# Feed-forward products: low parts of weights on VectorE alone, explicit order on all engines, a bank's steps between the next bank's weight tiles

## The chip, the cores and the metric

One core of one Trainium2 chip runs the whole program in one launch. The metric is the device time of that launch in microseconds: the median of three runs before is 1933.09 us (1932.76 to 1934.46).

## The reference

Two blocks over 256 tokens of 1024 features, batch 1, all in fp32. The first block has four layers, each with an attention (differential, stick-breaking, sliding window, differential) and a feed-forward with a causal convolution of three taps; it ends with a norm. The second block has a gated feed-forward, a mixing layer, an attention over a memory of 256 rows, and a second gated feed-forward. The parts that the change touches:

```python
def conv_gated_ffn(h, w_up, conv_w, conv_b, w_down):      # D_FF = 2752, layers 0 to 3
    u = h @ w_up                                          # [256, 2 * 2752]
    u = causal depthwise conv of width 3 over the tokens (u, conv_w) + conv_b
    gate, val = jnp.split(u, 2, axis=-1)
    return (jax.nn.silu(gate) * val) @ w_down

def swiglu(h, w_gate, w_up, w_down):                      # D_FF_2 = 2816, second block, twice
    return (jax.nn.silu(h @ w_gate) * (h @ w_up)) @ w_down
```

The input of each is a root-mean-square norm of the residual, and the first block's output is added to the residual `x = x + conv_gated_ffn(...)`.

## The kernel before

**Products.** Activations lie feature-major: 8 row tiles of 128 features by 256 tokens. Each fp32 product is made of three matmuls in a rounded format (`fp32r`): with weights w = hi + lo and activations a = ah + al, it sums hi·ah, hi·al and lo·ah (`fm`, L177). A *weight tile* is 128 x 128, so a weight tile is three matmuls of 256 columns. A *unit* is 8 weight tiles (128 x 1024 in SBUF), a *chunk* two units, 1 MB of the weight stream in DRAM, which is laid out in the order of use: 564 units in all.

**The weight stream.** `take` (L159) hands out tiles; at the middle of each unit it calls `split_to` for the unit three ahead (`AHEAD`), that is 20 tiles before its first use. `split_next` (L139) makes the high part `whi` with a copy on ScalarE (L153) and, a number of tiles later (`lag`, 4), the low part `wlo` with a subtraction (L156) on the engine that the string `lo_engines` names in turn: V for VectorE, P for GpSimd. The high and the low parts have 5 buffers each, the chunks 4; `dma_to` issues the transfer of a chunk on the sync queue (SP) three chunks ahead of the one that is split.

**Side work.** `spawn` puts a generator on a list; each number that it yields says how many weight tiles are to pass before its next step, and `tick`, called after every tile, runs the steps that are due. So the place of a step in the program is set in tiles of TensorE's work.

**Order on the engines.** `order()` (L1176) opens a region: without an argument every engine (the sync queue too) runs its instructions in the order of the program; with `{PE}` TensorE alone does, and a planner in the compiler places the instructions of the other engines by its own costs. Before, everything was explicit up to the last part of layer 0's attention output (`out_proj`) and from the cross-attention's output to the lead of the last feed-forward; the rest, all feed-forwards but that lead, had TensorE alone in explicit order.

**A feed-forward layer** (`ffn_layer`, L709). The up part has 22 *banks* of PSUM (`ubank`, three buffers): bank i holds the gate and value columns i, two products of 256 tokens, 16 weight tiles; bank 21 is one column (64 gate and 64 value features), 8 tiles. Banks 0 and 21 come first and advance together, row tile by row tile (the *lead*, 24 tiles), while the last row tiles of the normed input are being made. The norm's factor r comes by `start_norm`: after 12 tiles a product with a matrix of ones sums the squares `accss` over the partitions, and two activations on ScalarE make r. For each bank VectorE takes it out of PSUM times r (`ub`, L741), ScalarE starts the convolution (`y`, L746, once for gate and once for value), VectorE adds two taps to each (L748, four instructions), ScalarE does the silu (`gs`, L255), VectorE the product `g` (L755), ScalarE its high part `gh` (L759), VectorE its low part `gl` (L761). In the program these stand in one row after the bank's matmuls. The down part (`down`, L774) has 8 columns of 22 tiles, the first two together; row tile 21 has 64 rows and needs two matmuls, with high and low part stacked. Each column is added to the residual and goes through `feed` (L334) into the next layer's input. `lo_engines` is "VP" in the up part and "VVP" in the down part.

**The gated feed-forwards** (`swiglu`, L784) are alike, without taps, 22 banks of 16 tiles and 22 row tiles in the down part; "VVP" throughout. Beside the first, the memory is loaded and normed (`load_mem`, L1208); `final_r` (L1158) makes the factors of the norms. The last one's down part (`finish`, L860) is token-major.

Of the kernel before, what the change touches and what calls it, by code (L numbers as in the profile page):

```python
# [10 lines left out]
F32 = mybir.dt.float32  # L11
F32R = mybir.dt.float32r
AF = mybir.ActivationFunctionType
# [6 lines left out]
P = 128  # L20
T = 256
# [9 lines left out]
# Attention layers: weight tiles passed before the scores and before each later step of a block, the engines of the low  # L31
# parts of the weights, of the high copies of q and k, and of the other parts of q and of k.
# [40 lines left out]
class Act:  # L73
    """Activations in high and low parts. A stacked row tile has 64 rows: h holds the high part above the low part."""
# [5 lines left out]
class Net:  # L80
    def __init__(self, tc, ctx, A):
# [27 lines left out]
        self.bt_bufs = 3  # L109

# [22 lines left out]
    def split_to(self, u):  # L133
        while self.n_split <= min(u, N_UNITS - 1):
            self.dma_to(self.n_split // 2 + 3)
            gen = self.split_next(1024, 4)
            self.spawn(gen, next(gen))

    def split_next(self, step, lag=0):  # L139
        """the next unit of weights, in high and low parts, step columns at a time"""  # L140
# [35 lines left out]
    # feature-major products, row tile by row tile: out[128 features, 256 tokens] += W[rows kt, cols]^T act[kt]  # L176
# [17 lines left out]
    # token-major products: out[t][128 tokens, 256 or 512 features]  # L194
# [47 lines left out]
    def pin(self):  # L242
        """One table set serves every Exp and Ln until the next Silu."""
# [65 lines left out]
    def start_norm(self, f=None, tok=False, delay=10):  # L309
        """r of the tokens (in self.r, times f in self.rq, by token in self.rtok), after some weight tiles"""  # L310
# [27 lines left out]
    def out_proj(self, name, idx, act, rows, evac, order=tuple(range(KT)), urgent=False):  # L338
        """The first six columns advance together, row tile by row tile, while the last heads finish."""
# [31 lines left out]
    # one block of two score rows [128, 2, 384] (query tiles 0: 128 keys, 1: 256 keys)  # L371
# [10 lines left out]
    def q_parts(self, pool, ps):  # L382
        """[:, j]: the high part of head j in its own 64 rows, the low part in the other 64"""
# [13 lines left out]
    def k_parts(self, pool, ps, tag="", bufs=2):  # L397
        """the high part of head j in both halves of [:, j], and the low parts of both heads"""
# [15 lines left out]
    def head_product(self, out, j, q, queries, k, keys, keys_first=False):  # L414
        """queries x keys of head j (or keys x queries)"""
# [37 lines left out]
    def transposed(self, pool, a, ps):  # L453
        """a [128 q, 384] -> psum [128 k, 384]: keys 0..127 of 256 queries, keys 128..255 of queries 128.."""
# [3 lines left out]
    def load_bias(self, pool, kind, chans):  # L458
        """[query i, channel, key c]: bias at distance 128 + i - c"""
# [17 lines left out]
    # differential attention, one head  # L477
# [48 lines left out]
    # stick-breaking attention, a block of two heads  # L526
# [45 lines left out]
    # plain softmax attention with a Toeplitz bias, a block of two heads  # L572
# [55 lines left out]
    def units(self, name, idx, cols, act, kts=tuple(range(KT)), rows=None):  # L628
        """several output blocks, each in its own bank, advancing together"""
# [80 lines left out]
    def ffn_layer(self, layer, xf, nxt):  # L710
# [3 lines left out]
        with ExitStack() as st:  # L714
# [6 lines left out]
            for t in ub:  # L721
                nc.gpsimd.memset(t[:, :, 0:2], 0.0)
            self.lo_engines = "VP"
            self.start_norm(delay=12)
# [3 lines left out]
            self.fm([(b[:, p * T:p * T + T], name, layer, cols, p == 0)  # L728
                     for b, parts in zip(banks, lead) for p, cols in enumerate(parts)], xf, range(KT))
            for n, i in enumerate(order):  # L730
                parts = up_cols(i)
                np_ = len(parts)
                if n < 2:
                    bank = banks[n]
                else:
                    bank = self.ubank()
                    for p, cols in enumerate(parts):
                        self.fm([(bank[:, p * T:p * T + T], name, layer, cols, True)], xf, range(KT))
                r = self.r
# [10 lines left out]
                m = P if np_ == 2 else 64  # L750
# [15 lines left out]
            self.lo_engines = "VVP"  # L766
# [17 lines left out]
    def swiglu(self, tag, xt, rget, down):  # L784
        """down(g) takes the last product."""
        nc = self.nc
        with ExitStack() as st:
# [5 lines left out]
            self.lo_engines = "VVP"  # L793
# [6 lines left out]
            if self.manual:  # L800
                self.order({mybir.EngineType.PE})
# [529 lines left out]
```

## Time and profile before

| what | value |
|---|---|
| runs | 1932.76, 1933.09, 1934.46 us |
| span of the profiled execution, first to last instruction | 1932.7 us (its mean granted TensorE clock 0.980) |
| TensorE matmuls busy | 1849.3 us, 96%, 14082 instructions |
| weight loads (PEld) busy | 1761.5 us, 91% |
| VectorE (DVE) busy | 1342.0 us, 69% |
| ScalarE (ACT) busy | 1096.4 us, 57% |
| GpSimd (POOL) busy | 735.3 us, 38% |
| DMA | 314.87 MB, mean 163 GB/s |

Busy shares are means over the whole span, over stages with different limits. A matmul's record is longer than the distance to the next start, since matmuls are pipelined; the pace is read from the starts. "Idle before" an instruction is put down to what ended it.

### The profile page before, as it was taken

To read this page: it belongs to the slowest core of one execution; us is meant where nothing else is said; L and a number is where in the kernel's file an instruction comes from. 1 tells how busy PE (TensorE), PEld (TensorE's weight loads), DVE (VectorE), ACT (ScalarE), POOL (GpSimd) and SP (SyncE) were. 2 spreads that over 40 slices of the span, in tenths; PEclk is the share of its full clock that TensorE was granted. 3 is DMA by queue.
4 is the path that set the end of the run, shared out by engine and by line. 5 is a ranking of instruction groups with operands and counts; after the bars stand their busy time and mean duration, and the time that the engine had idled before them with its cause. 6 is when DMAs were issued, how large, how long until landed. Compare 5 with 4: busy or idle time off the path is not lost.

```text
span 1932.7 us, 35139 instructions
## 1 busy us (share of the span) xinstructions
PE 1849.3 (96%) x14082; PEld 1761.5 (91%) x14082; DVE 1342.0 (69%) x2093; ACT 1096.4 (57%) x1906; POOL 735.3 (38%) x433
## 2 busy tenths in 40 slices
PE   8999999999998999999999999989999999989998
PEld 7889989988987988999899899889999999989996
DVE  6778884676899557788757689967763655756653
ACT  6665664666555556566556655555544545655543
POOL 5453333554333321433344343334323454342222
PEclk9999999999998999999999999999999999999999
DMA  8634445433444452344544344454555454434452
GB/s 279 225 132 167 170 167 195 153 109 131 150 152 157 175 180 83 139 169 173 196 175 153 131 148 151 150 185 172 200 176 195 150 189 154 153 121 175 175 182 79
DMA packets 56994, 314.87 MB, mean 163 GB/s; under 512 B 5616, under 2 KB 19344, under 8 KB 20992
## 3 DMA queue, kind: packets, MB, share of 16 engines
q1 hardware_dynamic: 55872, 310.84, 45.4%
q8 instruction: 111, 1.82, 0.4%
q0 software_dynamic: 384, 1.04, 0.1%
q10 hardware_dynamic: 576, 0.75, 0.1%
q14 instruction: 51, 0.42, 0.1%
HBM read 311.52 MB, written 5.29 MB: 164 GB/s over the span
## 4 chain that ended last, share of the span: by engine, by line
PE 44%; DVE 10%; ACT 2%; issue 1%; POOL 1%; DVEq 0%; ACTq 0%; POOLq 0%
PE u L174 41%; DVE y L748 4%; PE s L174 3%; DVE wlo L156 2%; DVE ub L741 1%; DVE xtl L271 1%; ACT whi L153 1%; DVE x L836 1%; DVE g L755 0%; ACT gh L759 0%; ACT y L746 0%; DVE f L835 0%; PE s L456 0%; POOL wlo L156 0%; DVE accss L287 0%
## 5 line engine op out<-in xcount | busy, mean ns | idle before, releaser
L156 POOL TENSOR_TENSOR wlo<-stage,whi 128x1024 fp32r<-128x1024 f32 x245 | 598.1, 2442 | 1039.3 <-ACT whi L153 938.3
L174 PE MATMUL u<-xth,wlo 128*128 128x256 f32 x2704 | 776.8, 287 | 17.8 <-DVE wlo L156 9.5
L174 PE MATMUL u<-xth,whi 128*128 128x256 f32 x2704 | 782.7, 290 | 3.0 <-ACT xth L270 2.9
L174 PE MATMUL u<-xtl,whi 128*128 128x256 f32 x2704 | 770.5, 285 | 3.2 <-DVE xtl L271 3.2
L153 ACT ACTIVATE whi<-stage 128x1024 fp32r<-128x1024 f32 (+1 forms) x568 | 591.0, 1045 | 289.7 <-PE u L174 224.8
L156 DVE TENSOR_TENSOR wlo<-stage,whi 128x1024 fp32r<-128x1024 f32 (+1 forms) x323 | 420.2, 1303 | 204.7 <-ACT whi L153 201.9
L174 PEld LDWEIGHTS u<-xth,wlo 128*128 128x128 f32 x2704 | 523.9, 194 | 30.0 <-DVE wlo L156 18.0
L174 PEld LDWEIGHTS u<-xth,whi 128*128 128x128 f32 x2704 | 524.5, 194 | 9.5 <-ACT xth L270 3.3
L174 PEld LDWEIGHTS u<-xtl,whi 128*128 128x128 f32 x2704 | 524.5, 194 | 4.5 <-DVE xtl L271 3.6
L748 DVE SCALAR_TENSOR_TENSOR y<-ub,vec,y 128x256 f32<-128x256 f32 x344 | 276.1, 846 | 32.9 <-ACT y L746 29.3
L174 PE MATMUL u<-gh,whi 128*128 128x256 f32 x880 | 256.1, 291 | 18.3 <-DVE ub L741 18.3
L174 PE MATMUL u<-gh,wlo 128*128 128x256 f32 x880 | 255.9, 291 | 0.7 <-DVE wlo L156 0.7
L174 PE MATMUL u<-gl,whi 128*128 128x256 f32 x848 | 241.6, 285 | 0.0
L174 PEld LDWEIGHTS u<-gh,whi 128*128 128x128 f32 x880 | 169.6, 193 | 23.9 <-DVE ub L741 19.1
L174 PEld LDWEIGHTS u<-gh,wlo 128*128 128x128 f32 x880 | 168.8, 192 | 6.1 <-issue 1.6
L174 PEld LDWEIGHTS u<-gl,whi 128*128 128x128 f32 x848 | 163.2, 193 | 0.0
L746 ACT ACTIVATE y<-ub,vec 128x256 f32<-128x256 f32 x172 | 93.7, 593 | 39.3 <-DVE ub L741 39.3
L174 PE MATMUL u<-oh,whi 128*128 128x256 f32 x384 | 112.3, 292 | 1.4 <-DVE x L367 1.0
L174 PE MATMUL u<-ol,whi 128*128 128x256 f32 x384 | 108.2, 282 | 2.1 <-DVE ol L523 2.0
L174 PE MATMUL u<-oh,wlo 128*128 128x256 f32 x384 | 108.2, 282 | 0.0
L759 ACT ACTIVATE gh<-g 128x256 fp32r<-128x256 f32 x88 | 36.8, 418 | 103.7 <-DVE g L755 100.6
L271 DVE SCALAR_TENSOR_TENSOR xtl<-x,vec,xth 128x256 fp32r<-128x256 f32 x88 | 79.9, 913 | 18.8 <-ACT xth L270 18.7
(235 smaller groups left out, 2457.9 us busy)
## 6 DMA issues: line engine op xcount, KB each, us to landing
stage<-w SPq DMA_DIRECT2D x280, 1024.0 KB, 4.8
bt<-bt_d SPq DMA_DIRECT2D x24, 256.0 KB, 5.2
bt_d<-rows_d SPq DMA_DIRECT2D x1, 2048.0 KB, 12.2
stage<-w SPq DMA_DIRECT2D x4, 256.0 KB, 6.5
stage<-w SPq DMA_DIRECT2D x2, 512.0 KB, 7.0
bt_d<-rows_d SPq DMA_DIRECT2D x2, 512.0 KB
bt_d<-rows_d SPq DMA_DIRECT2D x1, 1024.0 KB
mem<-memT SPq DMA_DIRECT2D x8, 128.0 KB, 4.2
```

The source lines that it names most:

```text
L153: nc.scalar.activation(hi[:, s], src[:, s], AF.Copy)
L156: eng.tensor_tensor(lo[:, s], src[:, s], hi[:, s].bitcast(F32), OP.subtract)
L174: self.nc.tensor.matmul(out, lhsT, rhs, start=start, stop=stop, skip_group_check=True)
L271: nc.vector.scalar_tensor_tensor(l[:, j], src, gcol, h[:, j].bitcast(F32), op0=OP.mult, op1=OP.subtract)
L741: nc.vector.tensor_tensor(u[:, 0:np_, 2:258], bank[:, 0:np_ * T].rearrange("p (a t) -> p a t", t=T), r.unsqueeze(1).to_broadcast([P, np_, ...
L746: nc.scalar.activation(y[:, p], u[:, p, 2:258], AF.Identity, scale=cv(i, p, 2), bias=cv(i, p, 3))
L748: nc.vector.scalar_tensor_tensor(y[:, p], u[:, p, tap:tap + T], cv(i, p, tap), y[:, p], op0=OP.mult, op1=OP.add)
L759: nc.scalar.activation(gh[:m, i], g[:m], AF.Copy)
L836: nc.vector.tensor_tensor(self.x[:, c], self.x[:, c], self.f[:, c], OP.add)
```

## The change

The up and down parts of all six feed-forwards, and the leads, run in explicit order on all engines (`order()` at their start; after the down part TensorE alone again, save after the last). `lo_engines` is "V" in them, and `lag` is 6, back to 4 at their end. A bank's steps become a generator `gate`, spread over the next bank's tiles by its yields: for a layer `ub` at the bank's end, `y` after 2 tiles, the taps of the gate after 4, silu and the taps of the value after 5, `g` and `gh` after 9, `gl` after 13. Bank 0 starts as soon as r is there, bank 21 eight tiles after the lead. A layer's `start_norm` comes after 27 tiles, not 12. A row tile of the down part counts as done when its `gl` has been issued. Comments are left out of the changed file, so its line numbers differ.

```diff
+        self.lag = 4
-            gen = self.split_next(1024, 4)
+            gen = self.split_next(1024, self.lag)
...
 def ffn_layer(self, layer, xf, nxt):
-            self.lo_engines = "VP"
-            self.start_norm(delay=12)
+            self.order()
+            self.lo_engines = "V"
+            self.lag = 6
+            self.start_norm(delay=27)
...
+            def gate(n, i, bank):
+                np_ = len(up_cols(i))
+                m = P if np_ == 2 else 64
+                while self.r is None:
+                    yield 1
                 u = ub[n % 3]
                 nc.vector.tensor_tensor(
                     u[:, 0:np_, 2:258], bank[:, 0:np_ * T].rearrange("p (a t) -> p a t", t=T),
-                    r.unsqueeze(1).to_broadcast([P, np_, T]), OP.mult)
+                    self.r.unsqueeze(1).to_broadcast([P, np_, T]), OP.mult)
+                yield 2
                 y = pool.tile([P, 2, T], F32, tag="y", name="y")
                 for p in range(np_):
                     nc.scalar.activation(y[:, p], u[:, p, 2:258], AF.Identity, scale=cv(i, p, 2), bias=cv(i, p, 3))
+                def taps(p):
                     for tap in (1, 0):
                         nc.vector.scalar_tensor_tensor(y[:, p], u[:, p, tap:tap + T], cv(i, p, tap), y[:, p],
                                                        op0=OP.mult, op1=OP.add)
+                yield 2
+                taps(0)
+                yield 1
                 gs = pool.tile([P, T], F32, tag="gs", name="gs")
                 self.silu(gs[:m], y[:m, 0])
+                if np_ == 2:
+                    taps(1)
+                yield 4
...
                 nc.scalar.activation(gh[:m, i], g[:m], AF.Copy)
+                if n == 21:
+                    self.pin()
+                yield 4
                 low = gl[:, i] if np_ == 2 else gh[64:, i]
                 nc.vector.tensor_tensor(low, g[:m], gh[:m, i].bitcast(F32), OP.subtract)
-            self.pin()
+                ga.done.add(i)
+            def start(n, i, bank, delay=0):
+                gen = gate(n, i, bank)
+                if delay:
+                    self.spawn(gen, delay)
+                else:
+                    self.spawn(gen, next(gen))
...
+                    start(n, i, bank)
+                else:
+                    start(n, i, banks[n], 8 * n)
-            self.lo_engines = "VVP"
...
             self.down("ffn_w_down", layer, ga, order, after, rows)
+            self.lag = 4
+            self.order({mybir.EngineType.PE})
 def down(self, name, idx, act, order, after, rows=None):
-        act.done.update(range(22))
 def swiglu(self, tag, xt, rget, down):
-            self.lo_engines = "VVP"
+            self.order()
+            self.lo_engines = "V"
+            self.lag = 6
...
+            def gate(i, bank):
+                while self.r is None:
+                    yield 1
...
+                yield 3
                 gs = pool.tile([P, T], F32, tag="gs", name="gs")
                 self.silu(gs, u[:, 0])
+                yield 3
...
-            if self.manual:
-                self.order({mybir.EngineType.PE})
...
             down(ga)
+            self.lag = 4
+            if tag != "ffn2":
+                self.order({mybir.EngineType.PE})
 def finish(self, act, out):
                 parts = self.take(4)
+                while kt not in act.done:
+                    self.tick(True)
```

## Rows read from the trace of the kernel before

**Rows 1.** The core: us of the span, mean granted TensorE clock.
```profile
core 0: 1932.7 us, clock 0.980
```

**Rows 2.** Windows: us, busy and count by engine, clock, DMA; layers 0-3, gated, lead.
```profile
139.44:340.66 201.22, 193.32 (x1557) 189.25 (x1555) 149.81 (x209) 116.40 (x175) 77.35 (x38) 0.99 0.49 171
469.90:688.10 218.20, 201.44 (x1557) 193.54 (x1555) 166.45 (x209) 117.06 (x177) 76.28 (x39) 0.96 0.45 160
783.79:989.18 205.39, 196.51 (x1557) 192.03 (x1555) 154.15 (x209) 116.99 (x177) 77.93 (x39) 0.97 0.46 165
1114.63:1330.20 215.57, 200.31 (x1557) 192.45 (x1556) 169.21 (x211) 119.00 (x181) 79.11 (x42) 0.98 0.45 162
1335.63:1521.98 186.35, 186.35 (x1555) 186.35 (x1554) 113.03 (x132) 96.16 (x144) 61.05 (x31) 1.00 0.52 186
...
1726.35:1746.48 20.13, 16.96 (x91) 16.40 (x92) 15.16 (x21) 8.51 (x18) 10.12 (x9) 0.67 0.31 105
```

**Rows 3.** Waits: who waited for whom, us in total, times, longest.
```profile
PE u L174 <- DVE ub L741: 18.3, 4, 5.3
...
PE s L174 <- DVE accss L287: 15.4, 7, 4.0
...
PE u L174 <- DVE wlo L156: 11.0, 28, 1.6
```

**Rows 4.** Timeline of TensorE, layer 1, end of up part: start, us, what, idle.
```profile
614.39 0.38 PE L174 MATMUL u<-gh,wlo 128*128 128x256 f32 x1 [0.34 <-DVE wlo L156]
620.12 0.58 PE L174 MATMUL u<-gh,whi 128*128 128x256 f32 x1 [5.34 <-DVE ub L741]
620.50 0.41 PE L174 MATMUL u<-gl,whi 128*128 128x256 f32 x1
620.71 0.41 PE L174 MATMUL u<-gh,wlo 128*128 128x256 f32 x1
620.93 0.41 PE L174 MATMUL u<-gh,whi 128*128 128x256 f32 x1
```

**Rows 5.** Timeline of VectorE, layer 1, one bank of the up part and more.
```profile
564.58 1.23 DVE L156 TENSOR_TENSOR wlo<-stage,whi 128x1024 fp32r<-128x1024 f32 x1
565.72 3.83 DVE L748 SCALAR_TENSOR_TENSOR y<-ub,vec,y 128x256 f32<-128x256 f32 x4
569.65 0.43 DVE L755 TENSOR_TENSOR g<-gs,y 128x256 f32<-128x256 f32 x1
570.57 0.42 DVE L761 TENSOR_TENSOR gl<-g,gh 128x256 fp32r<-128x256 f32 x1 [0.48 <-ACT gh L759]
570.91 0.68 DVE L741 TENSOR_TENSOR ub<-u,r 128x512 f32<-128x512 f32 x1
571.51 1.23 DVE L156 TENSOR_TENSOR wlo<-stage,whi 128x1024 fp32r<-128x1024 f32 x1
572.66 1.27 DVE L748 SCALAR_TENSOR_TENSOR y<-ub,vec,y 128x256 f32<-128x256 f32 x3
```

**Rows 6.** Timeline of GpSimd, the same stretch.
```profile
566.88 2.39 POOL L156 TENSOR_TENSOR wlo<-stage,whi 128x1024 fp32r<-128x1024 f32 x1 [4.54 <-ACT whi L153]
```

**Rows 7.** Groups of ScalarE by line and form: busy, mean ns, idle before.
```profile
L153 ACT ACTIVATE whi<-stage 128x1024 fp32r<-128x1024 f32 x560 | 586.1, 1051 | 289.7 <-PE u L174 224.8 <-issue 53.1 <-ACT whi L153 3.6
L746 ACT ACTIVATE y<-ub,vec 128x256 f32<-128x256 f32 x172 | 93.7, 593 | 39.3 <-DVE ub L741 39.3
L759 ACT ACTIVATE gh<-g 128x256 fp32r<-128x256 f32 x84 | 35.2, 419 | 103.7 <-DVE g L755 100.6
L255 ACT ACTIVATE gs<-y 128x256 f32<-128x256 f32 x84 | 35.1, 418 | 74.1 <-DVE y L748 74.0
```

**Rows 8.** Timeline of TensorE, layer 1, the norm's ones-product.
```profile
478.20 1.22 PE L174 MATMUL s<-accss,ones 128*128 128x256 f32 x2 [3.82 <-DVE accss L287]
```

**Rows 9.** Timeline of TensorE, layer 1, the row tile of 64 rows.
```profile
639.38 0.28 PE L174 MATMUL u<-gh,whi 128*128 128x256 f32 x1
...
640.13 0.28 PE L174 MATMUL u<-gl,whi 128*128 128x256 f32 x1
```

More of the change, by code (lines that the diff above doesn't have):

```diff
@@ L727, in ffn_layer @@
             banks = [self.ubank(), self.ubank()]
[L728 to L739, printed above, removed]
+            def gate(n, i, bank):
[3 more added lines that the diff above has]
+                    yield 1
                 u = ub[n % 3]
@@ L749, in ffn_layer @@
                                                        op0=OP.mult, op1=OP.add)
-                m = P if np_ == 2 else 64
+                yield 2
+                taps(0)
+                yield 1
                 gs = pool.tile([P, T], F32, tag="gs", name="gs")
                 self.silu(gs[:m], y[:m, 0])
+                if np_ == 2:
+                    taps(1)
+                yield 4
                 g = pool.tile([P, T], F32, tag="g", name="g")
@@ L759, in ffn_layer @@
                 nc.scalar.activation(gh[:m, i], g[:m], AF.Copy)
+                if n == 21:
+                    self.pin()
+                yield 4
                 low = gl[:, i] if np_ == 2 else gh[64:, i]
                 nc.vector.tensor_tensor(low, g[:m], gh[:m, i].bitcast(F32), OP.subtract)
-            self.pin()
+                ga.done.add(i)
[5 more added lines that the diff above has]
+                    self.spawn(gen, next(gen))
+            self.fm([(b[:, p * T:p * T + T], name, layer, cols, p == 0)
+                     for b, parts in zip(banks, lead) for p, cols in enumerate(parts)], xf, range(KT))
+            for n, i in enumerate(order):
+                if n >= 2:
+                    bank = self.ubank()
+                    for p, cols in enumerate(up_cols(i)):
+                        self.fm([(bank[:, p * T:p * T + T], name, layer, cols, True)], xf, range(KT))
+                    start(n, i, bank)
+                else:
+                    start(n, i, banks[n], 8 * n)
             xn = self.new_act()
@@ L797, in swiglu @@
             banks = [self.ubank(), self.ubank()]
+            def gate(i, bank):
+                while self.r is None:
+                    yield 1
+                u = pool.tile([P, 2, T], F32, tag="u", name="u")
+                nc.vector.tensor_tensor(u, bank.rearrange("p (a t) -> p a t", t=T),
+                                        self.r.unsqueeze(1).to_broadcast([P, 2, T]), OP.mult)
+                yield 3
+                gs = pool.tile([P, T], F32, tag="gs", name="gs")
+                self.silu(gs, u[:, 0])
+                yield 3
+                g = pool.tile([P, T], F32, tag="g", name="g")
+                nc.vector.tensor_tensor(g, gs, u[:, 1], OP.mult)
+                nc.scalar.activation(gh[:, i], g, AF.Copy)
+                if i == 21:
+                    self.pin()
+                yield 3
+                nc.vector.tensor_tensor(gl[:, i], g, gh[:, i].bitcast(F32), OP.subtract)
+                ga.done.add(i)
             self.fm([(banks[i][:, p * T:p * T + T], names[p], 0, blk(i), p == 0) for i in range(2) for p in range(2)],
                     xt, range(KT))
-            if self.manual:
-                self.order({mybir.EngineType.PE})
             for i in range(22):
                 if i < 2:
-                    bank = banks[i]
+                    self.spawn(gate(i, banks[i]), 7 * i)
                 else:
@@ L808, in swiglu @@
                         self.fm([(bank[:, p * T:p * T + T], names[p], 0, blk(i), True)], xt, range(KT))
-                r = self.r
-                u = pool.tile([P, 2, T], F32, tag="u", name="u")
-                nc.vector.tensor_tensor(u, bank.rearrange("p (a t) -> p a t", t=T),
-                                        r.unsqueeze(1).to_broadcast([P, 2, T]), OP.mult)
-                gs = pool.tile([P, T], F32, tag="gs", name="gs")
-                self.silu(gs, u[:, 0])
-                g = pool.tile([P, T], F32, tag="g", name="g")
-                nc.vector.tensor_tensor(g, gs, u[:, 1], OP.mult)
-                nc.scalar.activation(gh[:, i], g, AF.Copy)
-                nc.vector.tensor_tensor(gl[:, i], g, gh[:, i].bitcast(F32), OP.subtract)
-            self.pin()
+                    gen = gate(i, bank)
+                    self.spawn(gen, next(gen))
             down(ga)
+            self.lag = 4
+            if tag != "ffn2":
+                self.order({mybir.EngineType.PE})
     def post_evac(self, gcol, late=False):
```

## The prediction

> **What bounds the kernel now.** First the span: 1932.7 us at a mean granted clock of 0.980 [rows 1]. The median of the runs shown is 1933.09 us, so some 0.4 us lie around the span; I work in the span and add that at the end. TensorE is busy 96% of it, so the question is which microseconds of the other engines reach TensorE, and only a stage by stage view tells that.
>
> So next the windows, one for each feed-forward product with its weights [rows 2]. The reader is to compare lines 1 to 4 (layers 0 to 3) with line 5 (first gated product of the second block). All are the same kind of work, three matmuls for each weight tile. Line 5 runs some 1555 matmuls in 186.35 us with TensorE busy all the time at clock 1.00: 0.120 us a matmul, 0.36 us a tile. A layer of lines 1 to 4 has 43 columns of 8 tiles in the up part (1032 matmuls) and 8 columns of 22 in the down part (528 less 8, since one row tile needs two), together 1552, which at 0.120 is 186.24 us. They took 201.2, 218.2, 205.4 and 215.6, together 840.4: 95.4 us more than 4 x 186.24 = 745.0. That is what the change can touch; line 6, the lead of the last feed-forward, has 20.1 us at clock 0.67 and is slow for another reason (below).
>
> Then the waits, for who makes TensorE idle [rows 3]: the `u` products wait for VectorE's `ub` (18.3 us in 4 times, once a layer), for VectorE's `wlo` (11.0 us, 28 times), and the ones-product for VectorE's `accss` (15.4 us in 7 times). All three are VectorE. The timeline of TensorE shows what such a wait costs besides itself: at the end of the up part of layer 1 it waits 5.34 us, and after it the matmuls come 0.22 us apart, not 0.12 [rows 4], until the granted clock is back: half speed for about three microseconds.
>
> Last, VectorE's own timeline in the middle of layer 1 [rows 5]. A bank (16 tiles, 48 x 0.12 = 5.76 us of TensorE) takes VectorE 6.94 us, from one pair `wlo`, `y` (564.58) to the next (571.51). The four `y` steps take 3.83 us. Three of them in the next period take 1.27 us, that is 0.40 apart. The difference is GpSimd: its `wlo` runs from 566.88 for 2.39 us [rows 6], in the middle of the slow four. So the low part put on GpSimd costs VectorE more (3.93 - 1.60 = 2.3 us) than computing it would (1.15 us, 571.51 to 572.66).
>
> **The change part by part.**
>
> *Low parts on VectorE alone.* A bank then has on VectorE, by start-to-start spacing in rows without GpSimd [rows 5]: `ub` 0.60 (570.91 to 571.51), two `wlo` at 1.15, four `y` at 0.40, `g` 0.42, `gl` 0.34 (570.57 to 570.91): 0.60 + 2.30 + 1.60 + 0.42 + 0.34 = 5.26 us against TensorE's 5.76. VectorE stops being the limit, with 0.50 us to spare. Added up by whole durations (0.68, 2 x 1.23, 4 x 0.48 with the last of the three at its full length, 0.43, 0.42) it is 5.9 us: that is the dear end, 0.15 us a bank over TensorE. I take 5.26, since the rows show the starts themselves. The down parts have 22 tiles, 7.9 us a column, for 2.75 `wlo` and three small steps: no limit either way.
>
> The Trainium skill (VectorE: DVE Perf Modes, The DRAIN you can't avoid) says that after every operation the pipe is flushed for about its duration less 266 ns before the next one starts. The trace does not agree: `wlo` of 1.23 us is followed by the next start after 1.15 [rows 5]. By the page's figure a bank would be near 9.4 us (an estimate); the rival it makes is priced below.
>
> *Explicit order and steps between tiles.* The order matters because every wait at the head of VectorE's or ScalarE's queue now holds all behind it. In tiles after the end of a bank, VectorE gets: `ub` at 0, `wlo` at 2, two `y` at 4, two at 5, `g` at 9, `wlo` at 10, `gl` at 13. ScalarE gets two `y` starts at 2, `whi` at 4, silu at 5, `gh` at 9, `whi` at 12: 2 x 1.05 + 2 x 0.59 + 0.42 + 0.42 = 4.1 us of 5.76 [rows 7]. The first `wlo` (1.15) stands over ScalarE's two `y` starts (1.2), the second pair of `y` steps (0.8) over the silu (0.42, behind a 1.05 `whi`, which began when `ub` was done), the second `wlo` over `gh` (0.42). The places where VectorE idled before, 0.48 us ahead of `gl` in each bank (570.57, behind `g` at 569.65) [rows 5], are filled. I cost the waits left at 0 to 0.3 us a bank, which the spare 0.50 covers; where it doesn't, a late `wlo` is next: it is issued 14 tiles, 5.0 us, ahead of its first use (lag 6 instead of 4 takes 0.7 us from that).
>
> *The end of the up part.* The down part's first banks wait no more for `ub`, which is now issued right at its bank's end and finds VectorE free: 18.3 us go [rows 3], with the half clock behind them, some 1.5 us each.
>
> *Norm at tile 27 instead of 12.* In layer 1 the ones-product waited 3.82 us and started at 478.20 [rows 8], 8.3 us after the lead's first matmul (469.90, the start of line 2 [rows 2]). Tile 27 is at 27 x 0.36 = 9.7 us: the sum is there. What is late next: the lead's last row tile, used at tile 21 (7.6 us), whose low part is made just ahead of that sum; 0 to 0.7 us a layer. Then VectorE waits for r at the head of its queue (about 1.5 us: the ones-product and two activations, each taken at the silu's 0.42 [rows 7]), with two banks' steps behind it: a backlog of 2 to 3 us, under the 5.0 us of lead of `wlo`. The third bank's successor needs the first bank's buffer only at tile 40.
>
> *What stays in a layer.* The row tile of 64 rows costs 0.39 us in each of 8 columns (639.38 to 640.13 is 0.75 for three spacings that cost 0.36) [rows 9]: 3.1 us. The two matmuls of the ones-product take some 0.6 (1.22 at half clock [rows 8]). So a layer becomes 186.2 + 3.1 + 0.6 + about 0.3 = 190.2 us, four 760.8, and 840.4 - 760.8 = 79.6 us are saved.
>
> *Gated products.* Line 5 is at TensorE's pace already [rows 2]: 0. VectorE was busy for 113 us of 186; it gets 22 low parts more (a third of 66 units, 25 us) and is held up by GpSimd less. ScalarE now waits in order for the memory tiles, each issued 2.9 us before its use; `whi` has 20 tiles of lead (7.2 us) over that. The last feed-forward's lead (line 6) waits on a chain of row steps; one GpSimd `wlo` fewer beside it is worth -3 to +2 us with the clock: I take -1.5.
>
> *Queues.* The sync queue gets the same transfers in program order; each weight chunk is asked for some 50 tiles (18 us) before use, and line 5 moves 186 GB/s at the pace that all layers would have. GpSimd keeps the squares' sums of the down part alone.
>
> Sum: 1932.7 - 79.6 - 1.5 = 1851.6 span, 1852 us as a run.
>
> **Rivals.**
>
> *VectorE just over TensorE.* If each operation starts only when the one before has ended, or in-order waits eat the spare, a bank is 5.9 to 6.1 us: 20 banks x 4 layers x 0.15 to 0.35 = 12 to 28 us back, 1864 to 1880. For it: the spare is a tenth, and eight steps a bank change engine. Against: the starts in rows 5, and the low parts placed where ScalarE works.
>
> *The other stages are planned anew.* The attention and mixing stages keep TensorE's order, but their other engines are placed by the planner, and its clock comes to them from a different past. They are 1932.7 - 840.4 - 2 x 190 = about 710 us; up to 2% of it either way, 14 us, gives 1838 to 1866. Nothing in the profile says which way.
>
> *Slower: one chain for a bank.* If the steps don't interleave, because `ub` at the queue's head waits for the bank's last matmul and every later step for ScalarE, a bank takes the whole chain: 0.68 + 1.18 + 1.92 + 0.42 + 0.43 + 0.42 + 0.42 = 5.5 us, and two `wlo` of 1.23 behind it, 7.9 us [rows 5, 7]. Then 80 banks x (7.9 - 5.76) = 173 us come back: 2025. It decides from 5.76 + 81/80 = 6.8 us a bank; the old order had 6.94 in layer 1. Against it stand the two `wlo` inside the chain, which need nothing of it.
>
> *The flush of every operation.* If each start on VectorE were held for as long again as the operation before it lasts, a bank would be 2 x 5.26 = 10.5 us, and 80 x 4.8 = 380 us more make 2230. The starts in rows 5 all but exclude it. (The rule is that of the Trainium skill's page VectorE: DVE Perf Modes, The DRAIN you can't avoid.)
>
> *The change doesn't do what it says*: if `y` stays at 3.83 us without GpSimd, a bank is 0.60 + 2.30 + 3.93 + 0.76 = 7.6 us, 1998. The 1.27 us for three [rows 5] is against it.
>
> **How the numbers follow.** Forecast (1842 to 1862): 0.66. VectorE just over: 0.16. Planned anew beyond 10 us: 0.12, half of it better. One chain, `y` still slow, the flush: 0.03, 0.01, 0.01; nothing gained because the order brings a wait of its own elsewhere: 0.01. Below, all 95.4 us gone would be 1837; above, the layers half way between 190 and layer 0's 201 of before give 1874, and some re-planning on top 1885. So 1838 to 1885 for 8 in 10. Two measurements of this kernel differ by up to 0.1%, and 0.2% (4 us) is what can be told from no change; faster 0.95, same 0.01, slower 0.04.
>
> **What would show it.** Right: banks of the up part 5.76 us apart in all four layers, windows of 189 to 191 us at clock 0.99 or more; no wait of `u` for `ub`, none of the ones-product over 1 us in a feed-forward; `y` at 0.40 spacing and no GpSimd `wlo` in these windows. Wrong: TensorE waiting for `wlo` in every bank (VectorE over its time), VectorE idle ahead of `y` or `g` for ScalarE more than 0.5 us a bank (the chain), or 190 us windows with a span over 1865 (lost in the other stages).

## The result and the profile after

| what | before | after |
|---|---|---|
| median of the runs shown together | 1933.78 us (1932.76 to 1934.58) | 1875.32 us (1872.12 to 1876.45) |
| ratio, 95% interval | | 0.9691 [0.9677, 0.9704] |
| span of the profiled execution, clock | 1932.7 us, 0.980 | 1870.3 us, 0.992 |
| four feed-forward layers | 840.4 us | 761.9 us |
| first gated feed-forward, up and down | 191.8 us | 216.4 us |
| memory keys, the stage behind it | 29.6 us | 25.3 us |
| last feed-forward, up part | 137.9 us | 133.9 us |

The kernel is 3.1% faster: 62.4 us of span. The layers give 78.5 us, the first gated feed-forward takes 24.6 back, the two stages under it in the table give 8.3, and all others, gains and losses added, 0.2. (Stages run from the first matmul of one to the first of the next; the times of up parts under the experiments end at the start of their last matmul, 0.12 us sooner.) 1875 lies in the range of 1838 to 1885 but 23 us above the forecast (the profiled run, 1872.12, is the lowest of its four; its span is 18.7 us above the forecast span), and the windows say at once where. They are the four layers, then the gated feed-forward, then the last one's lead; the columns are those of [rows 2].

```profile
139.49:329.95 190.46, 189.94 (x1557) 187.56 (x1556) 152.61 (x238) 114.13 (x175) 7.62 (x9) 1.00 0.50 178
457.71:648.18 190.47, 189.94 (x1557) 187.56 (x1555) 153.76 (x237) 114.69 (x177) 9.97 (x11) 1.00 0.50 182
743.59:934.06 190.47, 189.94 (x1557) 187.56 (x1555) 154.13 (x239) 114.75 (x177) 6.08 (x9) 1.00 0.50 178
1059.51:1249.97 190.46, 189.93 (x1556) 187.55 (x1555) 154.80 (x238) 116.41 (x181) 10.97 (x14) 1.00 0.51 180
1249.97:1466.37 216.40, 200.10 (x1591) 198.17 (x1589) 119.33 (x159) 98.74 (x149) 8.39 (x10) 0.96 0.47 167
1668.21:1688.30 20.09, 17.46 (x124) 16.60 (x125) 16.79 (x26) 12.67 (x24) 7.62 (x8) 0.92 0.30 106
```

The reader is to see that the four layers are alike to a hundredth and at clock 1.00, where they differed by 17 us in [rows 2], that GpSimd's busy time fell from some 77 us to under 11 in each, and that the fifth line, TensorE's full pace in [rows 2], is now the slow one. Next the waits of TensorE: `ub` is gone from the list, `accss` has 1.2 us where [rows 3] had 15.4, and one waiter stays, with more than before.

```profile
PE u L175 <- DVE wlo L157: 20.7, 15, 3.1
...
PE s L175 <- DVE accss L288: 1.2, 2, 0.6
```

VectorE's timeline in layer 1, one bank, answers to [rows 5]:

```profile
504.57 0.68 DVE L739 TENSOR_TENSOR ub<-u,r 128x512 f32<-128x512 f32 x1
505.18 1.21 DVE L157 TENSOR_TENSOR wlo<-stage,whi 128x1024 fp32r<-128x1024 f32 x1
506.31 1.91 DVE L749 SCALAR_TENSOR_TENSOR y<-ub,vec,y 128x256 f32<-128x256 f32 x4
508.32 0.42 DVE L761 TENSOR_TENSOR g<-gs,y 128x256 f32<-128x256 f32 x1
508.67 1.22 DVE L157 TENSOR_TENSOR wlo<-stage,whi 128x1024 fp32r<-128x1024 f32 x1
509.80 0.42 DVE L770 TENSOR_TENSOR gl<-g,gh 128x256 fp32r<-128x256 f32 x1
510.14 0.69 DVE L739 TENSOR_TENSOR ub<-u,r 128x512 f32<-128x512 f32 x1
```

Seven starts without one idle time: 5.57 us from `ub` to `ub`, under TensorE's 5.76. `y` takes 1.91 us for four, not 3.83, and not the 1.6 that I took. Taken singly, its four steps start at 506.31, 506.82, 507.22 and 507.74: the second and the fourth, which read what the step right before them wrote, start 0.51 us after it, the third 0.40.

Now the gated stage. Its waits on the other engines, and on SP's queue (SPq):

```profile
DVE mtl L272 <- ACT mth L271: 31.8, 8, 5.0
...
ACT mth L271 <- DMA mem<-memT: 26.1, 8, 4.6
```

```profile
SPq L128 <- DVE wlo L157: 201.6, 34, 11.3
```

And one turn of the loop that they form, in four timelines: SP (its issues alone), ScalarE, VectorE, TensorE.

```profile
1262.20 0.38 SPq L1254 DMA_DIRECT2D mem<-memT  x1
1272.40 0.33 SPq L128 DMA_DIRECT2D stage<-w  x1
1272.78 0.43 SPq L1254 DMA_DIRECT2D mem<-memT  x1
1281.99 0.33 SPq L128 DMA_DIRECT2D stage<-w  x1
1282.37 0.42 SPq L1254 DMA_DIRECT2D mem<-memT  x1
```

```profile
1277.58 0.51 ACT L271 ACTIVATE mth<-mem,vec 128x256 fp32r<-128x256 f32 x1 [1.94 <-DMA mem<-memT]
```

```profile
1278.12 0.48 DVE L272 SCALAR_TENSOR_TENSOR mtl<-mem,vec,mth 128x256 fp32r<-128x256 f32 x1 [2.41 <-ACT mth L271]
...
1280.71 1.22 DVE L157 TENSOR_TENSOR wlo<-stage,whi 128x1024 fp32r<-128x1024 f32 x1
```

```profile
1281.98 0.39 PE L175 MATMUL u<-xth,wlo 128*128 128x256 f32 x1 [3.08 <-DVE wlo L157]
```

Read it from the top. SP holds the weight chunk `stage` until VectorE's `wlo` has freed its buffer; the memory tile's transfer stands right behind it on the same queue and is issued at 1272.78, not when the program came to it. It lands 4.8 us later (median of the eight; 4.7 to 6.3). ScalarE stands in front of `mth` until 1277.58, with the next `whi` and `gh` behind it; VectorE stands in front of `mtl` until 1278.12, with `g`, `u` and the next `wlo` behind that. That `wlo` ends at 1281.9, TensorE waits 3.08 us for it, and so does SP's next chunk (1281.99), with the next memory tile behind it. Sixteen tiles, 5.76 us of TensorE, take 9.2 us a turn, until the eight memory tiles are through. Nine such waits in this stage make 16.3 of the 20.7 us for `wlo`; behind them matmuls run at half clock for a while (0.96 in the window's mean).

### The profile page after: what moved, and what is told of

It is laid out like the page before. It is cut to its first block, busy times and chain, and to the rows that moved or that the text cites. A ratio compares the mean times of both kernels' runs of the same rounds, so it can differ in the third digit from the quotient of the medians.

```text
span 1870.3 us, 34737 instructions
## 1 busy us (share of the span) xinstructions
PE 1820.4 (97%) x14082; PEld 1745.2 (93%) x14082; DVE 1322.4 (71%) x2254; ACT 1085.4 (58%) x1906; POOL 344.4 (18%) x272
## 5 line engine op out<-in xcount | busy, mean ns | idle before, releaser
L157 DVE TENSOR_TENSOR wlo<-stage,whi 128x1024 fp32r<-128x1024 f32 (+1 forms) x484 | 602.4, 1258 | 114.9 <-ACT whi L154 113.6
L154 ACT ACTIVATE whi<-stage 128x1024 fp32r<-128x1024 f32 (+1 forms) x568 | 583.8, 1042 | 111.3 <-PE u L175 97.0
L157 POOL TENSOR_TENSOR wlo<-stage,whi 128x1024 fp32r<-128x1024 f32 x84 | 204.4, 2436 | 354.5 <-ACT whi L154 317.8
L175 PE MATMUL u<-gh,wlo 128*128 128x256 f32 x880 | 251.7, 286 | 0.0
L175 PE MATMUL u<-gh,whi 128*128 128x256 f32 x880 | 251.0, 285 | 0.0
L288 POOL TENSOR_TENSOR accss<-accss,sq 128x256 f32<-128x256 f32 x60 | 58.0, 967 | 703.5 <-ACT sq L283 700.1
L175 PEld LDWEIGHTS u<-gh,wlo 128*128 128x128 f32 x880 | 164.9, 187 | 4.3
L749 DVE SCALAR_TENSOR_TENSOR y<-ub,vec,y 128x256 f32<-128x256 f32 x344 | 159.2, 482 | 9.5 <-ACT y L745 3.3
L271 ACT ACTIVATE xth<-x,vec 128x256 fp32r<-128x256 f32 x88 | 44.3, 504 | 123.0 <-DVE x L795 88.1
```

The costliest lines, as they stand in the source:

```text
L154: nc.scalar.activation(hi[:, s], src[:, s], AF.Copy)
L157: eng.tensor_tensor(lo[:, s], src[:, s], hi[:, s].bitcast(F32), OP.subtract)
L175: self.nc.tensor.matmul(out, lhsT, rhs, start=start, stop=stop, skip_group_check=True)
L271: nc.scalar.activation(h[:, j], src, AF.Copy, scale=gcol)
L288: eng.tensor_tensor(self.acc[key], self.acc[key], sq, OP.add)
```

## Experiments

All were timed in three rounds beside the kernel before; ratios are against it. The first three ask what the gated stage lost, the next five what the layers gained, the last three what follows from both.

**The memory tiles' transfers issued earlier.** Everything else as in the changed kernel:

```diff
-                for j in range(KT):
+                def get(j):
...
+                ms = [get(0)]
+                yield 16
+                for j in range(KT):
+                    if j + 1 < KT:
+                        ms.append(get(j + 1))
                     yield 8
...
-            self.spawn(load_mem(), 30)
+            self.spawn(load_mem(), 14)
```

> The changed kernel with each memory tile's transfer issued 24 weight tiles before its use instead of 8; the uses stay where they are. Theory A (the first gated feed-forward lost 24.6 us because ScalarE, in explicit order, stands at its queue's head for a memory tile that is still on its way, with whi, wlo and then the next weight transfer behind it): the wait of mth for mem, 26.1 us, goes below 3, and the stretch of the gated products falls from 216.4 to 190 to 193 us; the run 1848 to 1852 us. Rival B (explicit order of VectorE and ScalarE as such is too tight in this stage, with 22 low parts more on VectorE): the stretch stays above 205, the run above 1864.

Measured: 1847.24 us (1846.92 to 1848.43), ratio 0.9548 [0.9534, 0.9562]. The gated feed-forward's window and the idle time behind the memory tiles:

```profile
1250.69:1441.62 190.93, 190.93 (x1590) 190.83 (x1589) 119.55 (x159) 98.00 (x149) 8.46 (x10) 1.00 0.53 189
```

```profile
  ACT mth L271: 5.0, 8
```

No idle time of ScalarE ends with the transfer any more (26.1 us in 8 times in the changed kernel), `mtl` waits 5.0 us in place of 31.8, and the window has TensorE busy from end to end. The up part takes 127.5 us, not 152.9. The late transfer was the whole of the loss.

**The memory tiles' transfers from ScalarE's queue**, at the same place in the program:

```diff
-                    nc.sync.dma_start(out=m, in_=self.A["memT"][:, j])
+                    nc.scalar.dma_start(out=m, in_=self.A["memT"][:, j])
```

> The changed kernel with the memory transfers issued from ScalarE's queue instead of the sync queue, at the same place in the program (8 tiles before use). Theory A1 (what is too late is the issue: the memory transfer stands behind a weight transfer that waits on the sync queue for a low part): the transfer goes out 2.9 us ahead of its use and takes 4 to 6 us, the wait left is 1 to 3 us for each of 8, which the 7.2 us lead of whi covers; the stretch 190 to 195 us, the run 1847 to 1855. Theory A2 (8 tiles are too few from any queue): some 2 us stay for each tile, the stretch 200 to 212, the run 1860 to 1871. Rival B: no change, 1875.

Measured: 1847.57 us, ratio 0.9550; up part 127.9 us. The 8 tiles of lead are enough when the transfer is off SP's queue: it lands in 2.4 us (median), and ScalarE waits for it once, 2.0 us. What cost the time was the place behind a chunk that waits. That place makes the issue late and, 4.8 against 2.4 us, the landing too; this run does not part the two, but in the run before the landing still took 4.8 us and did no harm, since the issue was early.

**The first gated feed-forward with TensorE alone in explicit order**, its low parts still on VectorE:

```diff
-            self.order()
+            if tag == "ffn2":
+                self.order()
```

> The changed kernel with the first gated feed-forward ordered on TensorE alone, the other engines placed by the planner, everything else of the change kept there (low parts on VectorE, lag 6, steps spread). Theory A: a planner can put whi ahead of the use of a memory tile; the stretch is 190 to 194 us as before the change (191.8), the run 1848 to 1853. Rival B' (the low parts on VectorE alone cost it, not the order): above 205 us, the run above 1864.

Measured: 1847.96 us, ratio 0.9550; up part 127.5 us. The low parts on VectorE cost this stage nothing; the written order, with the transfer at the place that it had in it, did.

**Lag 4** in place of 6, in all feed-forwards of the changed kernel:

```diff
-            self.lag = 6
+            self.lag = 4
...
```

> The changed kernel with lag 4 instead of 6 in the feed-forwards: a low part may start 4 tiles after its high part. Theory: VectorE has 0.2 us to spare in a bank and TensorE does not wait for it in the layers, so nothing changes there (190.5 us each); in the first gated feed-forward the low part moves ahead by 0.7 us, and the sync queue with it, 0 to 3 us less. 1872 to 1876. Rival (lag 6 is what lets ScalarE be late without holding VectorE): each layer 1 to 4 us longer, 1879 to 1891.

Measured: 1996.16 us, ratio 1.0317 [1.0300, 1.0334]: slower than the kernel before, and off both expectations. The up parts of the layers take 153.0 us in place of 124.9 (153.3 in the last); the gated stage is some 8 us shorter, at 208.3, where I expected 0 to 3. VectorE in layer 1:

```profile
540.11 1.23 DVE L157 TENSOR_TENSOR wlo<-stage,whi 128x1024 fp32r<-128x1024 f32 x1 [0.53 <-ACT whi L154]
541.26 0.69 DVE L739 TENSOR_TENSOR ub<-u,r 128x512 f32<-128x512 f32 x1
542.67 1.92 DVE L749 SCALAR_TENSOR_TENSOR y<-ub,vec,y 128x256 f32<-128x256 f32 x4 [0.73 <-ACT y L745]
544.51 1.22 DVE L157 TENSOR_TENSOR wlo<-stage,whi 128x1024 fp32r<-128x1024 f32 x1
545.65 0.42 DVE L761 TENSOR_TENSOR g<-gs,y 128x256 f32<-128x256 f32 x1
546.55 0.42 DVE L770 TENSOR_TENSOR gl<-g,gh 128x256 fp32r<-128x256 f32 x1 [0.48 <-ACT gh L765]
547.50 1.23 DVE L157 TENSOR_TENSOR wlo<-stage,whi 128x1024 fp32r<-128x1024 f32 x1 [0.53 <-ACT whi L154]
```

The work is the same; the low parts now stand ahead of `ub` and ahead of `g` instead of behind them. So nothing lies over ScalarE's `y` (0.73), `gh` (0.48) and `whi` (0.53): 1.74 us of waits, 7.39 us a bank. Two tiles of lag decide 28 us in each up part, by what stands next to what on VectorE.

**GpSimd's low parts back in the up parts**, the order as changed:

```diff
-            self.lo_engines = "V"
+            self.lo_engines = "VP"
...
+            self.lo_engines = "V"
             self.down("ffn_w_down", layer, ga, order, after, rows)
```

> The changed kernel with every other low part of the up parts back on GpSimd (lo_engines VP), explicit order and spread steps kept. Theory (GpSimd's 2.4 us low part stops VectorE's tap steps while it runs): a bank of VectorE goes from 5.57 us to 5.57 - 1.14 + 1.4 to 2.3 = 5.8 to 6.7 us, over TensorE's 5.76; each layer is 3 to 18 us longer, the run 1885 to 1945; y takes up to 3.8 us for four. Rival (the explicit order alone made the gain, the engine of the low parts is nothing): layers stay at 190.5, the run at 1875.

Measured: 1943.12 us, ratio 1.0044 [1.0028, 1.0060]: as a run, no gain is left. Part of that is the gated stage, which stays as slow as in the changed kernel (218.4 us, against 216.4); the layers take 829.3 us, so 11.1 of their 78.5 us remain. VectorE and GpSimd in layer 1, and the last of VectorE's four steps by itself:

```profile
566.74 3.93 DVE L749 SCALAR_TENSOR_TENSOR y<-ub,vec,y 128x256 f32<-128x256 f32 x4
...
568.17 2.50 DVE L749 SCALAR_TENSOR_TENSOR y<-ub,vec,y 128x256 f32<-128x256 f32 x1
```

```profile
567.89 2.49 POOL L157 TENSOR_TENSOR wlo<-stage,whi 128x1024 fp32r<-128x1024 f32 x1 [4.54 <-ACT whi L154]
```

With GpSimd's low part inside them, the four steps take 2.0 us longer than the 1.92 without. All of it falls on the one step that starts while GpSimd's low part runs: it takes 2.50 us in place of 0.48 and ends at 570.67, just after the low part (570.38). In layers 0 and 2 that low part begins as `ub` runs (at 222.46 in layer 0), so part of it lies over VectorE's wait for `y`; there the steps take 2.80 us, the bank 6.13 and the up parts 133.2 and 133.8, against 147.8 here. The Trainium skill (SBUF — State Buffer, Who interferes with whom) has GpSimd share a pair of ports with VectorE operations that have two inputs in SBUF, taken by either for a whole instruction while the other is stopped. The trace agrees: one step is held for all that is left of a low part of 2.49 us, 2.0 us longer than it takes alone.

**The kernel before with the layers' low parts on VectorE**, and nothing else of the change:

```diff
-            self.lo_engines = "VP"
+            self.lo_engines = "V"
...
-            self.lo_engines = "VVP"
+            self.lo_engines = "V"
```

> The kernel before with one part of the change alone: low parts on VectorE in the layers' up and down parts, planner's order and the norm at tile 12 as before. Theory: the bank's pace of 5.76 us comes from this part, and the four layers lose at most the 53 us that they had above it in the up parts; the wait of the norm (4 us and its half clock) stays, and the wait for ub at the end of the up part becomes shorter: 1933 less 40 to 60 is 1873 to 1893. Rival (the explicit order is what does it): 1920 to 1935.

Measured: 1856.71 us (1855.92 to 1857.31), ratio 0.9593 [0.9578, 0.9607]: 4.1% from two strings, more than the whole change brought: the layers take 764.0 us, against 761.9 with the whole change, and the gated stage stays at 191.8. No `u` waits for `ub` any more, and the ones-products' wait is down to

```profile
PE s L174 <- DVE accss L287: 6.3, 6, 2.1
```

from 15.4 [rows 3], without any move of the norm.

**The norm at tile 12** in the changed kernel (`delay=27` to `delay=12`).

> The changed kernel with the norm's ones-product at tile 12 again. Theory: TensorE waits 3 to 4 us for accss in each layer and runs 2 to 3 us at half clock behind it, 4 to 6 us a layer, 16 to 24 us: 1891 to 1899. Rival (without GpSimd's low parts the sum of squares is ready earlier): 1 to 2 us a layer, 1879 to 1883.

Measured: 1872.96 us, ratio 0.9679 [0.9665, 0.9694], beside 0.9691 [0.9677, 0.9704]. The ones-product waits 3.5 us in 4 times, where it was 1.2 in 2 with tile 27, and the up parts take 124.1, 126.0, 125.1 and 124.5 us, beside 124.9: the move is worth nothing that these runs can tell. The traces say why. At tile 27 two waits in the layers, 2.4 us together, are gone; but VectorE's first `ub` then waits 3.6 to 5.2 us for r, where at tile 12 it waits 0.8 us for TensorE, and TensorE waits 0.53 us for a `wlo` behind that, once in each layer, 2.1 us together, of which there is none at tile 12.

**A bank's steps in one place.** In the layers' `gate` all yields between the steps are taken out (one remains at its end).

> The changed kernel with the steps of a layer's bank put one behind another at the bank's end, no tiles between. My rival of the prediction (one chain for a bank, 5.5 us, and two low parts behind it): 7.9 us a bank where TensorE needs 5.76, so some 173 us more, 2048. The other side: the chain holds VectorE for 5.5 us, but the low part that was queued ahead of it and ScalarE's high parts fill in, 6.5 to 7 us a bank, 60 to 100 us more, 1935 to 1975; if the spread is nothing, 1875.

Measured: 1988.4 us, ratio 1.0269 [1.0252, 1.0287]; up parts 151.7 us. VectorE in layer 1:

```profile
560.74 0.69 DVE L739 TENSOR_TENSOR ub<-u,r 128x512 f32<-128x512 f32 x1
562.15 1.92 DVE L748 SCALAR_TENSOR_TENSOR y<-ub,vec,y 128x256 f32<-128x256 f32 x4 [0.73 <-ACT y L744]
564.18 0.42 DVE L757 TENSOR_TENSOR g<-gs,y 128x256 f32<-128x256 f32 x1
565.09 0.42 DVE L765 TENSOR_TENSOR gl<-g,gh 128x256 fp32r<-128x256 f32 x1 [0.48 <-ACT gh L761]
565.43 2.35 DVE L157 TENSOR_TENSOR wlo<-stage,whi 128x1024 fp32r<-128x1024 f32 x2
567.70 0.68 DVE L739 TENSOR_TENSOR ub<-u,r 128x512 f32<-128x512 f32 x1
```

This is the rival of one chain for a bank: 6.96 us, the low parts at the end over nothing. It is shorter than the 7.9 I priced, because ScalarE's second `y` and its silu lie under VectorE's steps (some 0.45 and 0.3 us), and because on VectorE an operation that waits for nothing starts before the one ahead of it has ended: the second `wlo` and the next `ub` follow within 2.27 us, where I took 2 x 1.23.

**Lag 5, with the memory tiles early.**

> The changed kernel with the early memory transfers (1847.2 us), with lag 5 in place of 6 in all feed-forwards: the low parts land one tile after the bank's end and at tile 9, not at 2 and 10. Theory (what lag 4 cost was the place in VectorE's queue: a low part ahead of the bank's ub and one ahead of g leave nothing to lie over ScalarE's y and gh): at tile 1 the low part is behind ub and lies over the y starts as with lag 6, at tile 9 it may come just ahead of g or just behind; a bank's work of 5.6 us still fits TensorE's 5.76: 1846 to 1852 us, if ahead of g at most 0.5 us a bank more, 1885 us. Rival (it is the number of tiles between high and low part, or the lead, that counts): half way to the cost of lag 4 (1996 against 1875), 1905 to 1910 us.

Measured: 1848.08 us (1847.12 to 1848.85), ratio 0.9550 [0.9536, 0.9565], as with lag 6. The low parts still stand behind `ub` and behind `g`, and VectorE has no wait in a bank. With lag 4 this speaks for the order on VectorE and against the number of tiles: one tile less costs nothing, the next, which changes the order, 28 us in each up part.

**The convolution steps in turn, with the memory tiles early.** All four at tile 4:

```diff
-                def taps(p):
...
+                def taps(p, tap):
...
-                taps(0)
+                for tap in (1, 0):
+                    for p in range(np_):
+                        taps(p, tap)
...
-                if np_ == 2:
-                    taps(1)
```

> The changed kernel with the early memory transfers (1847.2 us); a bank's four convolution steps on VectorE stand together at tile 4, in the order gate, value, gate, value, so that no step reads what the one right before it wrote; before, both steps of one half stood behind each other. Theory (the 0.48 us a step in the changed kernel is the wait for the result of the step before; independent steps start 0.40 apart): four in 1.6 to 1.7 us instead of 1.92, a bank's work on VectorE 5.2 to 5.3 us instead of 5.57; TensorE paces the bank in both, so the time stays at 1846 to 1850 us. Rival (0.48 is what a step takes without GpSimd): 1.92 us again. Second rival: all four at tile 4 wait for ScalarE's second y with nothing to lie over it, 0.3 to 0.6 us a bank, of which some reaches TensorE: 1850 to 1890 us.

Measured: 1844.90 us (1844.82 to 1846.15), ratio 0.9536 [0.9520, 0.9552], the lowest of all. VectorE in layer 1, and the window of that layer:

```profile
541.95 0.69 DVE L739 TENSOR_TENSOR ub<-u,r 128x512 f32<-128x512 f32 x1 [0.35 <-PE u L175]
542.55 1.22 DVE L157 TENSOR_TENSOR wlo<-stage,whi 128x1024 fp32r<-128x1024 f32 x1
543.69 1.67 DVE L748 SCALAR_TENSOR_TENSOR y<-ub,vec,y 128x256 f32<-128x256 f32 x4
545.46 0.42 DVE L760 TENSOR_TENSOR g<-gs,y 128x256 f32<-128x256 f32 x1
545.80 1.22 DVE L157 TENSOR_TENSOR wlo<-stage,whi 128x1024 fp32r<-128x1024 f32 x1
546.93 0.42 DVE L769 TENSOR_TENSOR gl<-g,gh 128x256 fp32r<-128x256 f32 x1
547.70 0.69 DVE L739 TENSOR_TENSOR ub<-u,r 128x512 f32<-128x512 f32 x1 [0.35 <-PE u L175]
```

```profile
457.65:647.49 189.84, 189.84 (x1556) 187.56 (x1555) 150.81 (x237) 115.84 (x177) 9.96 (x11) 1.00 0.50 182
```

Four steps in 1.67 us, each 0.40 after the one before. In the changed kernel a step that read what the one right before it wrote started 0.51 after it, so the 0.48 of the expectation is the mean of four. The spare shows in how soon VectorE is level again after its wait for r: here a bank takes 5.32 us while it catches up, and from the 12th or 13th bank on it waits for TensorE, as above; in the changed kernel, at 5.57, it is level only in the last one to three of 22. I expected no change of time; the layer is 0.6 us shorter, because a wait of TensorE for `wlo` of 0.53 us some 24 us into each layer, where VectorE still works off what stood behind its wait for r, is gone. Four layers of that are the 2.3 us; the windows show it, while the intervals of the two ratios overlap.

**The kernel before with every feed-forward's low parts on VectorE**, by four strings alone: the layers' two, the one of the gated feed-forwards, and the one of the cross-attention (`xa`), which also holds for the first units of the last feed-forward and which the change leaves at "VVP".

> The kernel before with all low parts of all feed-forwards on VectorE (the layers' alone gave 1856.7 us), and nothing else. Theory (GpSimd's low parts hurt only where four convolution steps a bank share the ports; the gated products ran at TensorE's pace with them): the layers as with their low parts alone on VectorE, the gated parts within 2 us, the lead of the last feed-forward -3 to +1 us: 1852 to 1859 us. Rival (VectorE's load in the gated stages counts, since the planner of the compiler places it beside the memory's norm): the first gated up part 5 to 20 us longer than 128, 1862 to 1877 us.

Measured: 1850.03 us (1849.04 to 1850.65), ratio 0.9560 [0.9546, 0.9574], 2 us under my range. The gated up part is at 127.5 us and the last layer's window at

```profile
1062.17:1253.36 191.19, 189.95 (x1557) 187.56 (x1556) 153.51 (x239) 117.57 (x181) 10.27 (x14) 1.00 0.52 182
```

Beside the changed kernel with early transfers (1847.24 us), the written order, the spreading and the moved norm together are worth at most some 3 us, and the two intervals overlap (the string of `xa` differs between the two as well; no run has it alone). They are not free of use for that: once the order is written out, the spreading and the lag in it are worth over 100 us.

## Why the prediction was right, and where it was wrong

The forecast was 1852 us, and 1875 lies in the stated range. That is in part luck: the range reached up to 1885 for slower layers and for other stages planned anew, and neither cost anything here. What happened instead is the sign of being wrong that I had named last, windows of 190 us with a span over 1865, and it came from a term put at 0.

**Low parts on VectorE: right, and nearly all of the gain, with one term mis-sized.** The layers came to 761.9 us, forecast 760.8. With the strings alone in the kernel before they are at 764.1 (the four windows of the last experiment, added), and putting GpSimd back in the up parts took 67.4 of the 78.5 us away. The bank was 5.57 us against 5.26 forecast: the term of `y` was mis-sized. I took 0.40 us a step from [rows 5], where the even spacing suggests that the planner had put gate and value in turn; the change puts both steps of a half together, so that every other start comes after 0.51, and `g`, which reads the last of them, follows the first after 2.01, not 1.60. With the steps in turn the bank was 5.32, near the forecast. The step's sign held because 5.57 is still under 5.76; the spare was 0.19 us, not 0.50. The flush after each operation did not show, as the rows of before said: `wlo` of 1.21 us was followed by the next start after 1.13. The Trainium skill (VectorE: DVE Perf Modes, The DRAIN you can't avoid) adds in the same paragraph that a next operation which is not held starts earlier, which is what the starts here show. I had left that out, so the rival was priced from half of the rule.

**Explicit order and spreading: no waits, as costed, but not needed for the gain, and what keeps the waits away priced too low.** Of the layers' gain 2.2 us at most are theirs (764.1 against 761.9). I treated lag as 0.7 us of lead; lag 4 would have made 7.39 us a bank. I had placed the steps over ScalarE's work one by one in the text, and did not ask what one of them two tiles earlier would do.

**End of the up part: right, its price too low.** No `u` waits for `ub`. But the half clock behind that wait lasted longer than I read from [rows 4]. In layer 1 of the kernel before, the matmuls are 0.12 us apart again only here:

```profile
626.59 0.35 PE L174 MATMUL u<-gh,wlo 128*128 128x256 f32 x1
626.78 0.28 PE L174 MATMUL u<-gh,whi 128*128 128x256 f32 x1
626.90 0.28 PE L174 MATMUL u<-gl,whi 128*128 128x256 f32 x1
```

From 620.12 that is 6.5 us at half speed, not three, and some 3 us lost, not 1.5. The down parts, in which this wait lies, became 5.5, 9.0, 6.3 and 8.7 us shorter: 1.7 to 3.7 us more than the waits themselves. No term of the sum rests on this, since I built the layer up from its matmuls.

**Norm at tile 27: the wait went, but mostly not by the move.** In the layers the ones-product waited 13.6 us before, 4.6 with the two strings alone, 2.4 in the changed kernel with tile 12, and nothing with tile 27: it was GpSimd's low parts that made `accss` late. VectorE's wait for r was 3.6 to 5.2 us, not 1.5. The backlog behind it that I foresaw at 2 to 3 us was there, and it did reach TensorE, by 0.53 us a layer. The layer's 190.47 for 190.2 is that and little else.

**Gated products: wrong.** This step was put at 0 with "ScalarE now waits in order for the memory tiles, each issued 2.9 us before its use; `whi` has 20 tiles of lead (7.2 us) over that". It cost 24.6 us. I looked at ScalarE's queue and took the issue as made when the program reaches it; I did not write down SP's queue, where the transfer stood behind a chunk that waits for the very `wlo` which the late tile delays. The lead did not help, since the loop eats it within one turn. The part on queues said that the sync queue "gets the same transfers in program order" and left it at that. With that step mended (early or from another queue) the kernel runs 1847, 5 us under the forecast.

**Lead of the last feed-forward and the other stages.** I gave the lead 1.5 us; the up part gained 4.0 and the memory's keys 4.3, which stood in no term. The 4.0 us are in the lead: the 20.1 us from its first matmul on hold 124 matmuls in place of 91 [rows 2], at clock 0.92 in place of 0.67. In the kernel before with all strings on V both gains are there (memory keys 25.3 us, last up part 133.2), and with the layers' strings alone hardly (29.4 and 136.8), so they too come from GpSimd's low parts; by which wait was not followed.

## What to carry to other kernels

Before work is moved to a second engine for balance, look at what runs beside it on the first: here a low part on GpSimd cost VectorE 2.0 us where doing it took 1.13. When a planner's order is replaced by the program's, write down every queue, the one that issues transfers above all: here a transfer was issued only when all before it on its queue had gone, and a queue whose head waited for the consumer of its own late data closed a loop that cost 24.6 us. In a written order, put an instruction that needs nothing right behind one that another engine must answer, and check that place again when a distance changes.

## What the runs showed of the hardware

On VectorE, an operation of 128x256 that read what the one right before it wrote started 0.51 us after that one, others 0.40. Four of them took 1.92 us alone and 3.93 with one GpSimd operation of 2.49 us inside; the whole of the difference fell on the one step that started while GpSimd's operation ran. A transfer of one memory tile landed 4.8 us (median) after its issue from SP, behind a chunk of weights, and 2.4 us after its issue from ScalarE.
